# Half-row products on more array tiles, the gate in the sigmoid, five tiles ahead and turns at a bank

## The chip, the cores and the metric

One core of a Trainium2 chip runs the whole program. The metric is the time of one execution on the device, in microseconds (us). TensorE (PE) multiplies matrices, VectorE (DVE), ScalarE (ACT) and GpSimd (POOL) work element by element, and SyncE (SP) issues the transfers. Matrices stand in SBUF; products land in eight banks of PSUM, of 128 partitions by 512 numbers each.

## The reference

Two layers work on 512 tokens of 1024 numbers. Each has a mixer and a feed-forward, with norms, and with shifts, scales and gates that come from a condition vector. Layer 0's mixer is a sparse attention (an index product picks 128 keys per token); layer 1's is a state-space model. Cut to what matters here:

```python
x = x + g_m * mixer(h)                       # h = rms_norm(x) * (1 + scale) + shift
x = x + g_f * conv_ffn(h)

# mixer of layer 1: 64 groups of 16 channels, 64 complex states each, scanned along the tokens
bu = einsum('blgc,gpc->blgp', u, bb)
_, _, x_re, x_im = lax.associative_scan(...)
y = einsum(x_re, c_re) - einsum(x_im, c_im) + d_skip * u
g = gelu(y)
ga, gb = split(g @ w_glu)
out = ga * sigmoid(gb)

def conv_ffn(h):
    up = conv_along_tokens(h @ w_up, width=3) + conv_b     # 1024 -> 2 x 2816
    val, gate = split(up)
    return (silu(gate) * val) @ w_down
```

## The kernel before, in words

**Products.** The large products are made in three passes over operands that are split in a high and a low part (`mm3`: high x high, high x low, low x high); a row `acc<-wh,H` or `up<-H,wh` is of the first two, `wl` of the third. Small products are plain 32-bit ones; each of those matrix instructions leaves two records in the trace, so 16 matmuls are "x32" there.

**Order.** `Sched` (L172) writes the static order of every engine when the program is built. Tasks are generators that yield operations, spawned with a priority; `took` (L97) gives an operation's cost, `when` (L220) the time from which its operands are there in the scheduler's own model, from what `done` (L239) has noted of each region of a tile, and `run` (L322) picks, engine by engine, the operation that can start first, by priority. `Alt` names the same operation on two engines, and the scheduler takes the one where it ends sooner. Where the model sees PE idle for more than 1.6 us, `warm` (L751) puts in dummy products of the identity, tile `warm` in the trace. Nearly all instructions have the line of the scheduler's issue, L310, so they are told apart by tile names; `warm` has L759.

**Stages.** Attention: index product, selection, key and query products, 32 units (`unit`, L1062; tiles `S`, `s`, `pt`, `po`), output product. First feed-forward: `up` (L1202) makes one tile of 128 up-columns by 512 tokens in 24 matmuls; the first four tiles of a layer are taken together and in halves of 256 tokens, the first halves of all four before the second, since the norm's blocks of 128 tokens arrive one by one. Beside it run two side jobs of the SSM: `build_ops` (L1417) makes operators from the parameters, among them `kb`, a product of 64 rows by 32 columns per array tile, four tiles in one PSUM bank, with four copies `ks` on ACT.

**SSM.** `u_eight` gathers inputs (`pu`), `ssm_quarter` (L1740) makes for each of four quarters the inputs of the scan (`sre`), multiplies and scans them on DVE and POOL (`t`, `sre`) and leaves the states `X`. `ssm_out` (L1804) makes the outputs `py` of a quarter in two halves: a U part (8 matmuls) and an X part (16 matmuls on two array tiles of 64 x 64, one for each half of the rows); ACT takes gelu into `gy`, a gather `pg` turns it, and it becomes the operand H of the GLU. `load_states` (L1680) starts the loads for the quarters. `pre_ssm` (L1610), `scale_rows` (L1620) and `to_ssm` (L1636) bring the rows of a block through DRAM into the layout of the SSM.

**GLU.** Four products of 512 columns run in the order of `main` (L1873): gate half of the columns 0, value half 0, gate half 1, value half 1. `b_post` (L1850) takes the sigmoid of a gate block into `sg` on ACT. `a_post` (L1856) multiplies the value block by it on DVE, multiplies by the layer's gate vector on POOL, adds to x on DVE, and for the last columns starts the norm (`rs_v`, `rs_r`, `xn`) and the gathers `nt` of the second feed-forward's input H.

## Time and profile before

| | |
|---|---|
| median of 3 runs | 1280.53 us (1280.08 to 1280.97) |
| the profiled execution's own time | 1280.01 us |
| its span, first to last instruction | 1278.2 us |
| PE busy | 1252.0 us |
| DVE busy | 843.2 us |
| ACT busy | 520.6 us |
| POOL busy | 327.2 us |
| mean granted clock of PE | 0.995 |

The profile is one execution. A row of the timeline is a run of instructions of one kind on one engine: start, length, engine, line, operation, output<-input, shape, and how many records; in brackets how long the engine had been idle and what ended that. Ends of matmuls are modelled and overlap the next by a little, so the distance of two starts is the better measure. PE's granted clock is 1.00 at 2.4 GHz and 0.50 at 1.2 GHz.

### The profile page before, as it was taken

Reading aid. Unit: us, or ns where it says so; the run is one execution under the profiler, and the core shown is the slowest. Engines: PE = TensorE matmul, PEld = TensorE weight load, DVE = VectorE, ACT = ScalarE, POOL = GpSimd, SP = SyncE. Lnnn points to the kernel's source line nnn. Section 1 sums busy time; section 2 is a strip of 40 time slices with the busy share of each in tenths; the row PEclk is TensorE's granted clock in tenths of the full one; section 3 lists DMA queues with packets and bytes.
Section 4 is the critical chain, followed back from the end, with each engine's and each line's share of the span. In section 5 each row is a group of like instructions: output and inputs, shape, how many; then the busy total and the mean of one; then the engine's idle time right before and its main releaser. Section 6 shows DMA issues by size and latency. Waiting matters only on the chain. (4 is left out here: it accounts for less than half of the span.)

```text
span 1278.2 us, 19479 instructions
## 1 busy us (share of the span) xinstructions
PE 1252.0 (98%) x7264; PEld 989.7 (77%) x7264; DVE 843.2 (66%) x1602; ACT 520.6 (41%) x1121; POOL 327.2 (26%) x530
## 2 busy tenths in 40 slices
PE   7999999999999999999999999899999999999998
PEld 6766577666877678888888877788987888888886
DVE  6688697788677777768775378533686643666632
ACT  4345555556544334234443213423544432244420
POOL 0234446842144256343310304110200001000010
PEclk9999999999999999999999998999999999999999
DMA  9948521112386763444444669232443223322231
GB/s 375 365 162 316 179 85 64 53 34 67 118 304 242 245 237 113 143 176 144 153 126 177 158 197 372 91 104 77 165 137 138 97 91 124 114 77 77 81 99 48
DMA packets 76750, 195.68 MB, mean 153 GB/s; under 512 B 15204, under 2 KB 26084, under 8 KB 76656
## 3 DMA queue, kind: packets, MB, share of 16 engines
q1 hardware_dynamic: 73088, 191.52, 43.6%
q10 hardware_dynamic: 3568, 2.92, 0.8%
q8 instruction: 57, 0.93, 0.3%
q14 instruction: 37, 0.30, 0.1%
HBM read 172.10 MB, written 20.21 MB: 150 GB/s over the span
## 5 line engine op out<-in xcount | busy, mean ns | idle before, releaser
L310 PE MATMUL up<-H,wh 128*128 128x512 f32 (+1 forms) x1536 | 444.7, 374 | 0.0
L310 PEld LDWEIGHTS up<-H,wh 128*128 128x128 f32 x1536 | 277.7, 188 | 61.7 <-issue 12.1
L310 PE MATMUL up<-H,wl 128*128 128x512 f32 (+1 forms) x768 | 285.5, 372 | 0.0
L310 DVE TENSOR_TENSOR wl<-raw,wh 128x1024 fp32r<-128x1024 f32 (+1 forms) x192 | 234.2, 1227 | 65.5 <-ACT wh L310 59.4
L310 PE MATMUL acc<-wh,H 128*128 128x512 f32 (+3 forms) x752 | 241.1, 388 | 0.0
L310 ACT CAST wh<-raw 128x1024 fp32r<-128x1024 f32 (+1 forms) x192 | 192.7, 1015 | 109.9 <-DMA raw<-in_w_down_dram 45.8
L310 PE MATMUL acc<-wh,a 128*128 128x512 f32 x704 | 220.9, 392 | 0.0
L310 DVE SCALAR_TENSOR_TENSOR cv<-up,sm_b,cv 128x511 f32<-128x511 f32 (+1 forms) x176 | 131.6, 748 | 89.3 <-ACT cv L310 86.4
L310 PEld LDWEIGHTS acc<-wh,H 128*128 128x128 f32 x752 | 139.5, 189 | 44.2 <-issue 19.7
L310 PEld LDWEIGHTS up<-H,wl 128*128 128x128 f32 x768 | 144.6, 188 | 25.3
L310 PEld LDWEIGHTS acc<-wh,a 128*128 128x128 f32 x704 | 132.9, 189 | 27.8 <-issue 0.4
L310 ACT ACTIVATE cv<-up,sm_b 128x512 f32<-128x512 f32 x88 | 68.6, 780 | 197.5 <-PE up L310 180.0
L310 PE MATMUL acc<-wl,H 128*128 128x512 f32 (+3 forms) x376 | 141.7, 377 | 0.0
L310 POOL TENSOR_TENSOR x<-x,rt 128x512 f32<-128x512 f32 x20 | 31.5, 1578 | 415.7 <-DVE rt L310 407.6
L310 PE MATMUL acc<-wl,a 128*128 128x512 f32 x352 | 137.6, 391 | 0.0
L310 DVE TENSOR_TENSOR rt<-acc,gate 128x512 f32<-128x512 f32 x40 | 27.5, 689 | 101.0 <-PE acc L310 100.9
L310 PEld LDWEIGHTS acc<-wl,H 128*128 128x128 f32 x376 | 71.1, 189 | 10.2
L310 PEld LDWEIGHTS acc<-wl,a 128*128 128x128 f32 x352 | 66.4, 189 | 13.5
L310 POOL TENSOR_TENSOR rs_r<-rs_v,nhalf 128x1 f32<-128x1 f32 (+1 forms) x32 | 36.5, 1144 | 105.3 <-DVE rs_v L310 105.2
L310 ACT ACTIVATE cv<-cv 128x512 f32<-128x512 f32 x44 | 27.8, 632 | 68.5 <-DVE cv L310 68.5
L310 POOL TENSOR_TENSOR rm<-rm,rn 128x256 f32<-128x256 f32 (+3 forms) x46 | 37.2, 836 | 62.7 <-DVE rn L310 55.0
L310 PE MATMUL ada<-raw,cond_r 128*32 128x512 f32 (+1 forms) x544 | 49.2, 452 | 2.8 <-ACT xT L310 1.4
(268 smaller groups left out, 1512.9 us busy)
## 6 DMA issues: line engine op xcount, KB each, us to landing
raw<-in_ada_w_dram SPq DMA_DIRECT2D x96, 512.0 KB, 6.7
raw<-in_w_up_dram SPq DMA_DIRECT2D x88, 512.0 KB, 4.1
raw<-in_w_down_dram SPq DMA_DIRECT2D x40, 512.0 KB, 3.4
raw<-in_w_qkv_dram SPq DMA_DIRECT2D x24, 512.0 KB, 7.9
raw<-in_w_glu_dram SPq DMA_DIRECT2D x16, 512.0 KB, 9.6
k_d<-zq SPq DMA_DIRECT2D x8, 512.0 KB, 6.7
raw<-in_w_out_dram SPq DMA_DIRECT2D x8, 512.0 KB, 3.5
p_d<-p SPq DMA_DIRECT2D x16, 256.0 KB, 2.8
```

The source lines that it names most:

```text
L310: op.fn(*op.a, **op.k)
```

## The change

- **Costs of the scheduler.** A 32-bit product of 64 rows by at most 64 columns is priced at 0.55 of what it was. A PSUM bank that another engine reads counts as taken for readers of it until that read has ended (`when`, `done`, and `Res.get` with a fourth entry).
- **`kb`.** The 16 matmuls go to eight array tiles: two halves of the rows, each with a bank of its own, by four columns of 32. Eight copies of 32 x 128 follow instead of four of 32 x 256.
- **`py`.** Two banks instead of one, one for each half of the rows of the product; the outputs of neighbouring groups go to the two halves of the columns, so the X part has four 64 x 64 array tiles. Gelu comes in two instructions of 256 instead of one of 512. The rows of `w_glu` are laid out to match.
- **Gate.** The multiplication by the layer's gate vector moves from `a_post` to `b_post`, on POOL or DVE, onto the sigmoid.
- **Five tiles.** The first group of `up` has five tiles instead of four, in both layers.
- **Order of the SSM's start.** Sending the first half of a block's rows is a task of its own with a late priority, `scale_rows` of blocks 0 to 2 gets 2.5 instead of 0.8, and the states of quarters 0 and 1 are loaded under one rule.

```diff
@@ -108,6 +108,8 @@
             t = 0.013 + cols * 4.167e-4
         else:
             f = 1.0 if rhs.shape[0] > 64 and w > 64 else 0.285 if w <= 32 else 0.66
+            if rhs.shape[0] == 64 and w <= 64:
+                f *= 0.55
             if alone and f < 1:
                 f = 1.2
             t = max(0.056, f * cols * 4 * 4.167e-4 + 0.008)
@@ -222,8 +224,11 @@
         for aps, i in ((op.ins, 1), (op.outs, 2)):
             for ap in aps:
                 name, g = self.region(ap)
+
+                bank = ap.space == PSUM
                 for h, v in self.rec.get(name, {}).items():
-                    at = max(0.0 if op.e == v[2] == "PE" else v[0], v[1] if i == 2 else 0.0)
+                    at = max(0.0 if op.e == v[2] == "PE" else v[0],
+                             v[1] if i == 2 or bank and v[3] != op.e else 0.0)
                     if at > t and self.meet(g, h):
                         t = at
         return t
@@ -239,15 +244,15 @@
             name, g = self.region(ap)
-            v = self.rec.setdefault(name, {}).setdefault(g, [0.0, 0.0, ""])
-            v[1] = max(v[1], end)
+            v = self.rec.setdefault(name, {}).setdefault(g, [0.0, 0.0, "", ""])
+            v[1], v[3] = max(v[1], end), op.e
...
-            m[g] = [end, 0.0, op.e]
+            m[g] = [end, 0.0, op.e, ""]
@@ -1223,7 +1228,7 @@
         for half in range(2):
             i = 0
             while i < 2 * HT:
-                g = 4 if half == 0 and i == 0 else 1
+                g = 5 if half == 0 and i == 0 else 1
                 yield from up(2 * HT * half + i, g, 2 if g > 1 else 1)
                 i += g
                 flags.add(("up", layer, half))
@@ -1475,30 +1480,19 @@
                     tmp.put(Wt[h])
                     yield S.copy(p1[h].rearrange("p j i m -> p (j i m)"), pt)
                     sput(pt)
-                yield need(banks=1)
-                kb = sbank("kb")
-
-                ops = []
-                for ih in range(2):
-                    for i in range(2):
-                        for g2 in range(2):
-                            rows = slice(64 * g2, 64 * g2 + 64)
-                            for ip in range(2):
-                                ii = 2 * ih + ip
-                                jj = 4 * hq + ii
-                                qd = 64 * g2 + 32 * ip
-                                ops.append(PE.matmul(kb[qd:qd + 32, ih * P:(ih + 1) * P],
-                                                     bb[:, i].rearrange("p j c -> p (j c)")[rows, 16 * jj:16 * jj + 32],
-                                                     C[i][rows, ii, 0:8].rearrange("p k c -> p (k c)"),
-                                                     start=(i == 0), stop=(i == 1), tile_position=(64 * g2, qd)))
-                yield ops
+                yield need(banks=2)
+                kb = [sbank("kb") for _ in range(2)]
+
+                yield [PE.matmul(kb[g2][32 * ii:32 * ii + 32, :P],
+                                 bb[:, i].rearrange("p j c -> p (j c)")[64 * g2:64 * g2 + 64, 16 * (4 * hq + ii):16 * (4 * hq + ii) + 32],
+                                 C[i][64 * g2:64 * g2 + 64, ii, 0:8].rearrange("p k c -> p (k c)"),
+                                 start=(i == 0), stop=(i == 1), tile_position=(64 * g2, 32 * ii))
+                       for i in range(2) for ii in range(4) for g2 in range(2)]
                 jq = slice(4 * hq, 4 * hq + 4)
                 for g2 in range(2):
-                    for ip in range(2):
-                        qd = 64 * g2 + 32 * ip
-                        yield S.copy(ks[64 * g2:64 * g2 + 32, jq.start + ip:jq.stop:2],
-                                     kb[qd:qd + 32, :2 * P].rearrange("p (a b) -> p a b", a=2))
-                sput(kb)
+                    for ii in range(4):
+                        yield S.copy(ks[64 * g2:64 * g2 + 32, jq.start + ii], kb[g2][32 * ii:32 * ii + 32, :P])
+                sput(*kb)
                 spawn(store_ops(qt, jq, p1, C, ks, dB), 5.5)
 
     def ada1(*groups):
@@ -1613,6 +1607,9 @@
         yield need(tmps=1)
         xa = tmp.get("xa")
         yield Alt(*[E.tensor_mul(xa, x[:, b, :512], ROWS["a"][:, :512]) for E in (G, V)])
+        spawn(send_first(b, xa), 5.5)
+
+    def send_first(b, xa):
         yield DM(X8[0][16 * b:16 * b + 16], xa)
         tmp.put(xa)
         flags.add(("x0", b))
@@ -1640,7 +1637,7 @@
         r = yield from rstd_of(ss, 1, 1.0 / D, E0.pop(b))
-        spawn(scale_rows(b, r), 0.8)
+        spawn(scale_rows(b, r), 0.8 if b == NB - 1 else 2.5)
         yield V.scalar_tensor_tensor(xb, xb, r, ROWS["s"][:, 512:], op0=ALU.mult, op1=ALU.add)
@@ -1681,8 +1678,8 @@
             yield has(("built", q))
-            if q == 1:
-                yield lambda: WS.ns >= glu0 and len(U) and quad.free() >= 3
+            if q < 2:
+                yield lambda: WS.ns >= glu0 and len(U) >= 2 * q and quad.free() >= 3
@@ -1806,22 +1803,22 @@
         CA, Kt, own = OPS[q]
         for h in range(2):
             yield has(("x", q, h))
-            yield need(banks=1)
-            py = sbank("py")
+            yield need(banks=2)
+
+            py = [sbank("py") for _ in range(2)]
             js = range(4 * h, 4 * h + 4)
-            o = lambda j, g2: py[64 * g2:64 * g2 + 64, (j % 4) * P:(j % 4 + 1) * P]
-            ops = [PE.matmul(o(j, g2), U[q][:, 2 * j + g2], Kt[g2][:, j], start=(j == js[0]), stop=False,
-                             tile_position=(0, 64 * g2)) for j in js for g2 in range(2)]
-            for i in range(2):
-                for j in js:
-                    for g2 in range(2):
-                        r = slice(64 * g2, 64 * g2 + 64)
-                        ops.append(PE.matmul(o(j, g2), X[i][r, j], CA[i][r, j], start=False, stop=(i == 1 and j == js[-1]),
-                                             tile_position=(64 * g2, 64 * g2)))
-            yield ops
-            yield S.activation(gy[:, :, 4 * h:4 * h + 4].rearrange("p t j c -> p j t c"),
-                               py.rearrange("p (j t c) -> p j t c", j=4, t=8), AF.Gelu_apprx_tanh)
-            sput(py)
+            at = lambda j: 64 * (j % 2)
+            o = lambda j, g2: py[g2][at(j):at(j) + 64, j % 4 // 2 * P:(j % 4 // 2 + 1) * P]
+            yield [PE.matmul(o(j, g2), U[q][:, 2 * j + g2], Kt[g2][:, j], start=(j < js[2]), stop=False,
+                             tile_position=(0, at(j))) for g2 in range(2) for j in js]
+            r = [slice(64 * g2, 64 * g2 + 64) for g2 in range(2)]
+            yield [PE.matmul(o(j, g2), X[i][r[g2], j], CA[i][r[g2], j], start=False, stop=(i == 1 and j >= js[2]),
+                             tile_position=(64 * g2, at(j))) for i in range(2) for j in js for g2 in range(2)]
+            for g2 in range(2):
+                js_ = slice(4 * h + 2 * g2, 4 * h + 2 * g2 + 2)
+                yield S.activation(gy[:, :, js_].rearrange("p t j c -> p j t c"),
+                                   py[g2][:, :256].rearrange("p (j t c) -> p j t c", j=2, t=8), AF.Gelu_apprx_tanh)
+            sput(*py)
         flags.add(("y", q))
         quad.put(U[q])
         if own:
@@ -1847,19 +1844,24 @@
 
     sg = {}
 
-    def b_post(b, ps):
-        yield need(tmps=1)
-        sg[b] = tmp.get("sg")
-        yield S.activation(sg[b], ps, AF.Sigmoid)
-        bank.put(ps)
+    def b_post(ch):
+        def post(b, ps):
+            yield need(tmps=1)
+            s_ = tmp.get("sg")
+            yield S.activation(s_, ps, AF.Sigmoid)
+            bank.put(ps)
+
+            yield lambda: (1, 2) in gates
+            yield Alt(*[E.tensor_mul(s_, s_, gates[1, 2][:, ch * 512:(ch + 1) * 512]) for E in (G, V)])
+            sg[b] = s_
+        return post
 
     def a_post(ch, then):
         def post(b, ps):
-            yield lambda: b in sg and (1, 2) in gates
+            yield lambda: b in sg
             s_ = sg.pop(b)
             yield V.tensor_mul(s_, ps, s_)
             bank.put(ps)
-            yield G.tensor_mul(s_, s_, gates[1, 2][:, ch * 512:(ch + 1) * 512])
             xs = x[:, b, ch * 512:(ch + 1) * 512]
             yield V.tensor_add(xs, xs, s_)
             tmp.put(s_)
@@ -1973,12 +1975,12 @@
                     if k == KT - 1:
-                        spawn(b_post(b, acc[b]), 2)
+                        spawn(b_post(0)(b, acc[b]), 2)
...
         state["side_max"] = 3
         yield from gemm(KT, 512, gh[0], gh[1], a_post(0, None), tail=4)
-        yield from gemm(KT, 512, gh[0], gh[1], b_post, tail=4)
+        yield from gemm(KT, 512, gh[0], gh[1], b_post(1), tail=4)
         H1 = new_H()
@@ -2055,7 +2057,8 @@
-    wg = fp(f("ssm_w_glu")[0]).reshape(4, 8, 2, 16, 2, 2, 512).transpose(0, 2, 1, 3, 4, 5, 6).reshape(4, 2, 128, 2, 2, 512)
+    wg = fp(f("ssm_w_glu")[0]).reshape(4, 2, 2, 2, 2, 16, 2, 2, 512).transpose(0, 3, 1, 4, 2, 5, 6, 7, 8)
+    wg = wg.reshape(4, 2, 128, 2, 2, 512)
```

How the order moves, on PE, at three places. First the end of the SSM: the outputs `py` of quarter 2, the gathers `pg`, and the first GLU products `acc`. Before:

```order
L310 MATMUL pg<-sm_a,gy 128x128 x4
L310 MATMUL py<-XU,U 64x128 x8
L310 MATMUL py<-XU,X_8453 64x128 x8
L310 MATMUL py<-XU,X_8454 64x128 x8
L310 MATMUL ada<-raw,cond_r 32x512 x4
L310 MATMUL pg<-sm_a,gy 128x128 x4
L310 MATMUL acc<-wh,H 128x512
L310 MATMUL acc<-wl,H 128x512
L310 MATMUL acc<-wh,H 128x512 x2
L310 MATMUL acc<-wl,H 128x512
L310 MATMUL acc<-wh,H 128x512 x2
```

Now:

```order
L315 MATMUL py<-XU,U 64x128 x8
L315 MATMUL acc<-wh,H 128x512
L315 MATMUL acc<-wl,H 128x512
L315 MATMUL acc<-wh,H 128x512
L315 MATMUL py<-XU,X_8493 64x128 x8
L315 MATMUL py<-XU,X_8494 64x128 x8
L315 MATMUL pg<-sm_a,gy 128x128 x4
L315 MATMUL adat<-sm_a,rows 128x128 x4
L315 MATMUL acc<-wh,H 128x512
L315 MATMUL acc<-wl,H 128x512
L315 MATMUL acc<-wh,H 128x512
L315 MATMUL py<-XU,U 64x128 x8
```

GLU products, which stood behind both halves of quarter 2, now stand between its U and X parts. Up to the last `pg` of the stage there are 36 of them now and 30 before; behind that `pg` the change has a `warm` of 6.

Second, the passage from the GLU (`acc`) to the second feed-forward (`up`), with the gathers `nt` of the normed rows. Before:

```order
L310 MATMUL acc<-wh,H 128x512 x2
L310 MATMUL acc<-wl,H 128x512
L310 MATMUL acc<-wh,H 128x512
L310 MATMUL nt<-sm_a,xn 128x128 x4
L759 MATMUL warm<-sm_a 128x128 x17
L310 MATMUL up<-H,wh 128x256 x2
L310 MATMUL up<-H,wl 128x256
```

Now:

```order
L315 MATMUL acc<-wh,H 128x512
L315 MATMUL acc<-wl,H 128x512
L315 MATMUL acc<-wh,H 128x512 x2
L315 MATMUL acc<-wl,H 128x512
L315 MATMUL acc<-wh,H 128x512
L315 MATMUL nt<-sm_a,xn 128x128 x4
L315 MATMUL acc<-wh,H 128x512
L315 MATMUL acc<-wl,H 128x512
L315 MATMUL acc<-wh,H 128x512 x2
L315 MATMUL acc<-wl,H 128x512
L315 MATMUL acc<-wh,H 128x512
L315 MATMUL up<-H,wh 128x256 x2
```

Another gather stands in the row ahead of this piece. The last two gathers thus have six matmuls of the GLU behind each, where the last one had none, and no `warm` is left.

Third, the end of the attention's units: `S` are scores, `pt` transposes, `po` outputs, `acc<-wh,H` products of the input projection. Before:

```order
L310 MATMUL po<-pT,vt 64x128 x6
L310 MATMUL S<-kT,qT 128x512 x2
L759 MATMUL warm<-sm_a 128x128 x7
L310 MATMUL pt<-sm_a,s 128x128 x8
L310 MATMUL po<-pT,vt 64x128 x8
L310 MATMUL pt<-sm_a,s 128x128 x16
L310 MATMUL S<-kT,qT 128x512 x2
L310 MATMUL po<-pT,vt 64x128 x16
L310 MATMUL S<-kT,qT 128x128 x4
```

Now:

```order
L315 MATMUL acc<-wh,H 128x512
L315 MATMUL pt<-sm_a,s 128x128 x8
L315 MATMUL acc<-wh,H 128x512
L315 MATMUL acc<-wl,H 128x512
L315 MATMUL acc<-wh,H 128x512
L315 MATMUL po<-pT,vt 64x128 x8
L315 MATMUL pt<-sm_a,s 128x128 x8
L315 MATMUL acc<-wh,H 128x512
L315 MATMUL acc<-wl,H 128x512
L315 MATMUL acc<-wh,H 128x512
L315 MATMUL po<-pT,vt 64x128 x8
```

Products of the input projection reach down to here and stand between the transposes and the outputs. The `warm` of 7 is gone; one of 8 stands further up, within that projection.

## Rows read from the trace of the kernel before

**Rows 1.** Page, part 1: busy time, share of the span and instructions of each engine.
```profile
PE 1252.0 (98%) x7264; PEld 989.7 (77%) x7264; DVE 843.2 (66%) x1602; ACT 520.6 (41%) x1121; POOL 327.2 (26%) x530
```

**Rows 2.** Waits of PE over the span: us in total, times, longest.
```profile
PE pg L310 <- ACT gy L310: 3.6, 1, 3.6
...
PE po L310 <- DVE pT L310: 1.6, 5, 0.5
...
PE pt L310 <- DVE s L310: 1.4, 2, 0.9
```

**Rows 3.** Timeline, PE, three stretches: start, us, engine line op out<-in xcount [idle before].
```profile
250.52 1.83 PE L759 MATMUL warm<-sm_a 128*128 128x128 f32 x14
...
363.43 1.28 PE L759 MATMUL warm<-sm_a 128*128 128x128 f32 x10
...
906.35 3.96 PE L759 MATMUL warm<-sm_a 128*128 128x128 f32 x34
```

**Rows 4.** Windows: us, then PE, PEld, DVE, ACT, POOL busy (x), PEclk, DMA share, GB/s.
```profile
776.20:783.10 6.90, 6.90 (x62) 6.01 (x60) 5.00 (x8) 2.96 (x4) 1.42 (x4) 0.51 1.03 403
806.90:810.40 3.50, 2.96 (x9) 2.57 (x10) 3.41 (x5) 1.12 (x3) 2.80 (x2) 0.51 0.02 5
```

**Rows 5.** Timeline, PE, the SSM stage's end and the GLU's start.
```profile
780.50 3.17 PE L310 MATMUL py<-XU,X 64*64 64x128 f32 x32
...
807.44 1.12 PE L310 MATMUL pg<-sm_a,gy 128*128 128x128 f32 x4 [3.58 <-ACT gy L310]
...
825.76 0.40 PE L310 MATMUL acc<-wl,H 128*128 128x512 f32 x1
```

**Rows 6.** Timeline, PE, one `kb` group in the first feed-forward.
```profile
387.72 1.08 PE L310 MATMUL kb<-C,bb 64*32 64x128 f32 x32
388.72 0.73 PE L310 MATMUL up<-H,wh 128*128 128x512 f32 x2
```

**Rows 7.** Windows, of the first feed-forward and of the SSM stage.
```profile
380.00:440.00 60.00, 60.00 (x351) 42.10 (x350) 44.56 (x89) 24.52 (x37) 23.96 (x58) 1.00 0.73 240
785.50:800.00 14.50, 14.43 (x242) 11.68 (x238) 13.87 (x20) 5.36 (x9) 6.30 (x5) 1.00 1.03 402
```

**Rows 8.** Groups of instructions that read tile `kb`, on ACT: ns min/median/max, first and last start.
```profile
L310 ACT COPY ks<-kb x32: 344/364/367, 390.5 to 659.4; 32x256 f32<-32x256 f32 x32
```

**Rows 9.** Timeline, PE, `py` of quarter 3, first half.
```profile
813.23 1.09 PE L310 MATMUL py<-XU,U 128*64 128x128 f32 x16
814.26 1.96 PE L310 MATMUL py<-XU,X 64*64 64x128 f32 x32
816.15 0.66 PE L310 MATMUL adat<-sm_a,rows 128*128 128x128 f32 x4
```

**Rows 10.** Timeline, DVE, the SSM stage.
```profile
785.62 1.29 DVE L310 TENSOR_TENSOR t<-sre,T 128x512 f32<-128x512 f32 x2 [2.08 <-PE sre L310]
```

**Rows 11.** Timeline, POOL, X of quarter 3.
```profile
808.89 2.21 POOL L310 TENSOR_TENSOR X<-t,t 128x504 f32<-128x504 f32 x1 [0.63 <-DVE t L310]
```

**Rows 12.** Chain that ended last: start, us, engine tile line xcount.
```profile
895.80 0.44 PE nt L310 x4
...
963.28 70.95 PE up L310 x312
```

**Rows 13.** Timeline, POOL, then DVE, end of the GLU.
```profile
894.56 1.73 POOL L310 TENSOR_TENSOR sg<-sg,gate 128x512 f32<-128x512 f32 x1 [1.78 <-DVE sg L310]
...
896.32 0.69 DVE L310 TENSOR_TENSOR x<-x,sg 128x512 f32<-128x512 f32 x1 [1.18 <-POOL sg L310]
...
898.34 0.69 DVE L310 TENSOR_TENSOR H<-ht,H 128x512 fp32r<-128x512 f32 x1
```

**Rows 14.** Timeline, PE, the first `up` of layer 1.
```profile
910.07 0.48 PE L310 MATMUL up<-H,wh 128*128 128x256 f32 x2
...
910.50 0.40 PE L310 MATMUL up<-H,wh 128*128 128x256 f32 x2
...
910.86 0.40 PE L310 MATMUL up<-H,wh 128*128 128x256 f32 x2
```

More of the change, by code (lines that the diff above doesn't have):

```diff
@@ L391, in get @@
         ap = self.pool.tile(shape or [P, self.cols], dtype, tag=self.tag, bufs=self.n, name=name)
-        self.s.rec[ap.tensor.name] = {(0, P, 0, 1 << 40, ()): [at, 0.0, ""]}
+        self.s.rec[ap.tensor.name] = {(0, P, 0, 1 << 40, ()): [at, 0.0, "", ""]}
         return ap
```

## The prediction

> **What bounds the kernel now.** I read the page first: TensorE (PE) is busy 98% of the span and the other engines 66% or less [rows 1]. So two things can make the kernel shorter: PE executing its matmuls in less time, and PE no longer standing still. The table of waits says how little of the second is left by name: the longest after the start is 3.6 us before a gather `pg`, and the two entries of the attention's units come to 1.6 and 1.4 us over all 32 of them [rows 2]. But "busy" hides two more kinds of waste, so I read the timeline and the windows next. Padding: the scheduler puts `warm` matmuls where it foresees idleness; three of their rows, at 250, 363 and 906 us, come into the sum [rows 3]. Half clock: two stretches of the SSM stage have a granted clock of 0.51, which is the 1.2 GHz level [rows 4]; in the second, PE had just stood 3.58 us in front of `pg` [rows 5]. The durations below are taken from rows at the full 2.4 GHz where nothing else is said.
>
> The profiled execution took 1280.01 us, its span is 1278.2 and the median of the runs is 1280.53, so sums made against 1280.0 hold for the median within half a microsecond. Under 0.2% (2.6 us) a measurement of this kernel can't tell a difference from none.
>
> **Part 1, `kb` on eight array tiles.** Eight groups of 32 records run between products of the feed-forward. One starts at 387.72, and the next row starts 1.00 us later [rows 6]. Today four tiles work at a time: 8 steps of 125 ns. If eight tiles run together at that pace there are 4 steps, 0.5 us, and PE is the bound there, its windows full (60.00 of 60 us) [rows 7]. Taken: 0.45 us each, **-3.6** in all; bounds 0 (no more overlap) and -4.0. The four more copies per group go to ACT, 24.52 of 60 us busy there [rows 7], and are costed at nothing; without that cover a group's copies would be four more of the 0.36 us that one takes now [rows 8], at most 8 x 4 x 0.36 = 11.5 us, but only if PE had no `up` to go on with.
> The same row gives a second reading. 32 records in 1.00 us is 31 ns a record, and no group of the trace shows less. The Trainium skill, *TensorE: Matmul & The Clock Gate*, section "Wait — 56ns, not 53.3ns?", says that matmuls never start closer than about 25 ns apart, however small they are; no run here has shown that floor yet. By it (an estimate from that page) `kb` would end at 0.8 us and the term would be -1.6; it is a rival below.
>
> **Part 2, the end of the SSM and the GLU's start.** The X part of a half takes 1.89 us from 814.26 to 816.15 with two tiles at work, 59 ns a record [rows 9]. On four quadrants it is 32 records at `kb`'s four-tile pace of 31 ns [rows 6]: 1.0 us, 0.9 saved in each of eight halves. Only where PE is the limit does it count. In quarter 0 it does: `sre` of quarter 2 waits behind that product, and DVE waits 2.08 us for `sre` at 785.62 [rows 10]; from there it is 13.87 of 14.50 us busy up to 800 [rows 7], and what it does is the chain to quarter 3's X. The X of this half, at 780.50, ran at half clock and took 3.17 us [rows 4, 5], so 0.9 to 2.0 is gained, within the 2.08 that DVE has idle. X of quarter 3 is ready at 811.10 now (808.89 + 2.21, on POOL) [rows 11]; I take 809.5 to 811.1 for the change, middle 810.3.
> From there I count progress. Before, 30 GLU matmuls stand ahead of the stage's last `pg`, and the 36th is the row at 825.76, done by 826.0 [rows 5]. After, the order has all 36 ahead of that `pg`, 24 of them between quarter 2's products, where PE now stands for 3.58 us. What is left behind quarter 3's X: two X parts of 1.0, one U part (813.23 to 814.26 now, 1.0) [rows 9], twelve GLU matmuls at the 0.227 of a 512-column product [rows 12] (2.7), two `pg` of four records and 6 `warm` of two, 20 records at the 0.11 of `warm` (2.2): 7.9 us. The 36th is then done at 818.2: **-7.8**. The padding is part of it, and so is the half clock of rows 4, which the filled hole should prevent. Bounds: if DVE and POOL are the limit and a last gather waits for gelu as now, some 3 to 5 us of that comes back: -3; with X at 808.5, -10.
> `load_states` and the priorities only set the order of this stage. The 13 `warm` in place of 20 ahead of the first `sre` stand in a hole that a norm's chain sets: nothing.
>
> **Part 3, the gate in the sigmoid.** At the end of the GLU POOL multiplies a block by the gate in 1.73 us, and the sum on DVE waits for it until 896.32 [rows 13]. The first `up` starts at 910.07 [rows 14], behind the `warm` that starts at 906.35 [rows 3], 3.7 us (34 records, 0.11 each). The order of the change has no `warm` there: two gathers `nt` stand among the last GLU matmuls, then `up`. PE's work up to there is the same, so `up` can start at 906.35, **-3.7**. It needs the first half of block 1's H then, and the second after the first four steps of a tile (12 matmuls at 0.12: 1.4 us, 907.8). The last `nt` now comes 6 matmuls earlier, ends near 905.0, and from the end of the `nt` of 895.80 [rows 12] to the end of its H at 899.03 [rows 13] it is 2.8 us: 907.8. Just in time; if it is not, at most 1.4 comes back, so the bounds are -2.3 and -4. The multiply itself is hidden: it is done once the sigmoid is there, many microseconds ahead of the product that needs it, on POOL and DVE.
>
> **Part 4, five tiles ahead, twice.** The fifth tile's 24 matmuls of 512 become 48 of 256. Three halves take 0.36 us (910.50 to 910.86) [rows 14], so 0.12 each; a full one takes 70.95 / 312 = 0.227 [rows 12]. 24 x (0.24 - 0.227) = 0.3, in two layers **+0.6**. For that PE has 2.9 us more to do ahead of the second half of the columns: in layer 0 the 1.28 us of `warm` at 363.43 [rows 3] go, **-1.3**, bounds -1.3 and +1 (H late, a bare wait in its place); in layer 1 it is cover for part 3.
>
> **Part 5, turns at a bank.** The rule costs no instruction; it changes the order of the attention. Its `warm` of 1.83 us at 250.52 goes [rows 3], and 8 new ones (16 records x 0.11) come in the input projection: 0. The waits in the attention's units add to 3.0 us [rows 2]; I take half as gone, **-1.5**, bounds -3 and +5 (0.15 us more in each of 32 units). PE changes ten times more between the two kinds of product and back. A change costs little: `up` behind `kb` takes 0.57 us for two at 388.72 [rows 6] where 0.45 is the rule, so 0.1 a pair, **+1.0**.
>
> **Sum**: -3.6 - 7.8 - 3.7 + 0.6 - 1.3 - 1.5 + 1.0 = -16.3. I give 0.8 back for what the exact fits of parts 2 and 3 can miss: -15.5, **1264.5 us**.
>
> **The rivals.**
> A, *an issue floor*: small matmuls start no closer than some interval, whatever tiles they use. For it: no row shows less than 31 ns. Against: none of them had eight tiles to use. `kb` goes to 0.8 us, -1.6 in place of -3.6, X (31 ns) hardly changes: 1266.5. The skill's page has this rule. Chance 0.14.
> B, *tiles of one row half don't run together*: neither `kb` nor X changes its pace. For it: X is at 59 ns with two tiles, and nothing in the trace shows four 64x64 tiles. Against: `kb`'s four tiles stand at 31 ns. It costs 3.6 of part 1 and 1.8 (quarter 3) plus about 1 (quarter 0) of part 2: 1271. Chance 0.10.
> C, *the SSM stage is DVE's and POOL's*: the wait moves from `pg` to X of quarter 3 or the gather behind it, and the clock falls again. For it: DVE's 13.87 of 14.50 us [rows 7], POOL's 2.21 us for one X [rows 11]. Against: just before, DVE waits 2.08 us for PE [rows 10]. Part 2 gives 1.5 instead of 7.8: 1270.8. Chance 0.18.
> D, *slower*: the new order of the attention opens waits. The scheduler now believes in turns that the chip may not have, and puts a unit's products behind each other. Each unit would wait more than 15.5 / 32 = 0.48 us longer, at which point all gain is gone; at 0.6 it is +19: 1283.7. Against: all waits there are 3.0 us now, 0.1 a unit [rows 2], so they would have to grow sixfold. Chance 0.07.
> E, *nothing*: the tiles wait for each other as before and every hole moves on to the next engine, with the span half a microsecond shorter: 1279.5. For it: DVE's load. Against: the `warm` rows of 906 and 363 are bare PE time that the order no longer has. Chance 0.03.
>
> **How the numbers follow.** The forecast has 0.48. Faster by over 0.2% are it, A, B and C: 0.90, less 0.01 for ends of C: 0.89. E and the edges of C and D make the same: 0.05; slower: 0.06. The range: the low end takes the good bounds of parts 2 and 5 (2.2 and 1.5), `kb`'s 0.4 and some 3 us for attention and joins that fit better than I counted: 1257. The upper end takes in A, B and C with two to three more us: 1274. D and E are left out, with some 0.1 of tails.
>
> **What would show it.** `kb` rows: 0.5 us to the next row (A: 0.8, B: 1.0). X rows of `py`: 1.0 us for 32 records (B: 1.9). No 3.58 us in front of a `pg` and no clock of 0.51 around 808; the 36th GLU matmul 7.8 us nearer to the end of the first feed-forward than now (C: a wait of 3 us or more, before X or `pg`). No `warm` and no wait over 0.5 us between the last GLU matmul and `up`; none at the first feed-forward's join. The sum of PE's waits in 100 to 260 us under 5 us (D: over 15). The prediction is wrong if the attention's span up to 265 us grows by more than 5 us, or if the SSM stage from the end of the first feed-forward to the GLU's 36th matmul shrinks by less than 3.

## The result, and the profile after

The changed kernel takes 1267.42 us (median of 4 runs, 1265.99 to 1271.37), the kernel before 1280.75 (median of 4): a ratio of 0.9892, with a 95% interval of 0.9871 to 0.9912. That is 13 us faster; the time is 2.9 us above the 1264.5 that was forecast, and inside the range. The profiled execution took 1268.01 us, 12.0 less than the profiled one before, and it is those 12.0 that the stages below divide.

Two of the first lines of the changed kernel's page (compare [rows 1]):

```profile
span 1266.2 us, 19526 instructions
...
PE 1239.3 (98%) x7268; PEld 975.8 (77%) x7268; DVE 838.0 (66%) x1584; ACT 531.3 (42%) x1166; POOL 323.5 (26%) x545
```

PE is as full as before, with 12.7 us less to do. Where they went is read from the start of the same product in both profiles:

| from | to | before | after | difference | forecast |
|---|---|---|---|---|---|
| start | first `up` | 348.26 | 351.90 | **+3.6** | -1.5, and a part of the +1.0 for switches |
| first `up` | last product of the first feed-forward | 406.23 | 401.70 | -4.5 | -3.6 - 1.3 + 0.3 |
| there | 100th GLU product | 85.38 | 77.68 | -7.7 | -7.8 |
| there | first `up` of layer 1 | 70.20 | 67.00 | -3.2 | -3.7 |
| there | last product | 363.13 | 362.94 | -0.2 | +0.3 |

The products that bound the stages, on PE, before and then after (the first `up` of layer 1 before is in [rows 14], the one after stands further down):

```profile
348.26 0.40 PE L310 MATMUL up<-H,wh 128*128 128x256 f32 x2
...
754.49 0.40 PE L310 MATMUL acc<-wh,a 128*128 128x512 f32 x1
...
839.87 0.39 PE L310 MATMUL acc<-wh,H 128*128 128x512 f32 x1
...
1273.20 0.39 PE L310 MATMUL acc<-wh,a 128*128 128x512 f32 x1
...
351.90 0.40 PE L315 MATMUL up<-H,wh 128*128 128x256 f32 x2
...
753.60 0.39 PE L315 MATMUL acc<-wh,a 128*128 128x512 f32 x1
...
831.28 0.39 PE L315 MATMUL acc<-wh,H 128*128 128x512 f32 x1
...
1261.22 0.39 PE L315 MATMUL acc<-wh,a 128*128 128x512 f32 x1
```

Four stages came as forecast within half a microsecond; the first moved the other way. Here are the lines that show it. Waits of PE over the span (compare [rows 2]: `pg` had 3.6, `pt` 1.4):

```profile
PE pt L315 <- DVE s L315: 4.2, 2, 3.0
PE pu L315 <- DVE t L315: 3.5, 2, 3.1
...
PE pg L315 <- ACT gy L315: 1.4, 2, 1.1
```

The 3.6 us ahead of `pg` have shrunk, as expected, and a wait of 3.0 us in the attention is the new longest one. The timeline of PE there, and of DVE:

```profile
262.44 0.71 PE L315 MATMUL S<-kT,qT 64*128 64x128 f32 x8
266.11 2.22 PE L315 MATMUL pt<-sm_a,s 128*128 128x128 f32 x10 [2.96 <-DVE s L315]
...
262.86 1.22 DVE L315 TENSOR_TENSOR wl<-raw,wh 128x1024 fp32r<-128x1024 f32 x1
...
265.47 0.88 DVE L315 TENSOR_SCALAR s<-s,rsm 128x512 f32<-128x512 f32 x2
```

PE waits for the scaled scores `s`, which DVE makes at 265.47; a split of weights (`wl`) and four masks of the next units stand ahead of them on DVE. Windows of the changed kernel, behind that wait, in the SSM stage, and where the clock fell in [rows 4] at 806.90:

```profile
266.40:269.80 3.40, 3.40 (x23) 2.90 (x22) 1.96 (x6) 0.43 (x2) 1.19 (x2) 0.50 0.01 2
775.00:781.80 6.80, 6.80 (x80) 6.02 (x81) 3.68 (x6) 3.94 (x7) 0.82 (x3) 0.50 1.04 404
803.00:808.00 5.00, 4.12 (x33) 3.27 (x33) 5.00 (x9) 3.69 (x7) 3.19 (x2) 1.00 0.14 52
```

The half clock at 776 is still there, the one around 808 is gone, and one stands in the attention. The prediction counted two stretches of half clock before; there is a third, of 3.4 us, in the first feed-forward near 738, in both kernels. The rest of the profile answers to the forecast's steps. `kb` (compare [rows 6]), the SSM's end (compare [rows 5, 9]) and the passage to the second feed-forward (compare [rows 3, 14]), on PE:

```profile
394.64 0.67 PE L315 MATMUL kb<-C,bb 64*32 64x128 f32 x32
395.24 0.73 PE L315 MATMUL up<-H,wh 128*128 128x512 f32 x2
...
808.17 1.10 PE L315 MATMUL py<-XU,X 64*64 64x128 f32 x32
809.21 1.09 PE L315 MATMUL py<-XU,U 128*64 128x128 f32 x16
...
814.83 0.39 PE L315 MATMUL acc<-wh,H 128*128 128x512 f32 x1
815.06 0.60 PE L315 MATMUL pg<-sm_a,gy 128*128 128x128 f32 x4
815.50 1.50 PE L764 MATMUL warm<-sm_a 128*128 128x128 f32 x12
816.76 0.48 PE L315 MATMUL acc<-wh,H 128*128 128x512 f32 x1
...
898.05 0.40 PE L315 MATMUL acc<-wh,H 128*128 128x512 f32 x1
898.28 0.40 PE L315 MATMUL up<-H,wh 128*128 128x256 f32 x2
```

`kb` takes 0.60 us for 32 records, X 1.04. The 36th GLU product, at 814.83, is followed by a gather and the padding, and `up` begins 0.23 us after the last GLU product.

### The profile page after: what moved, and what is told of

The parts are those of the page before. It is cut to its first block, busy times and chain, and to the rows that moved or that the text cites. A ratio compares the mean times of both kernels' runs of the same rounds, so it can differ in the third digit from the quotient of the medians.

```text
span 1266.2 us, 19526 instructions
## 1 busy us (share of the span) xinstructions
PE 1239.3 (98%) x7268; PEld 975.8 (77%) x7268; DVE 838.0 (66%) x1584; ACT 531.3 (42%) x1166; POOL 323.5 (26%) x545
## 5 line engine op out<-in xcount | busy, mean ns | idle before, releaser
L315 PEld LDWEIGHTS up<-H,wh 128*128 128x128 f32 x1568 | 281.7, 189 | 61.4 <-issue 10.4
L315 PE MATMUL acc<-wh,H 128*128 128x512 f32 (+3 forms) x752 | 244.2, 389 | 0.0
L315 PEld LDWEIGHTS up<-H,wl 128*128 128x128 f32 x784 | 147.7, 188 | 24.6
L315 PEld LDWEIGHTS acc<-wh,a 128*128 128x128 f32 x704 | 132.9, 189 | 27.8 <-issue 0.2
L315 ACT ACTIVATE cv<-cv 128x512 f32<-128x512 f32 x44 | 27.8, 632 | 68.9 <-DVE cv L315 68.9
L315 POOL TENSOR_TENSOR rm<-rm,rn 128x256 f32<-128x256 f32 (+3 forms) x46 | 33.9, 763 | 59.0 <-DVE rn L315 57.9
```

Source lines behind the costliest of these rows:

```text
L315: op.fn(*op.a, **op.k)
```

## The experiments

Each run is compared by the stages of the table, each from one profile. Two profiles of the changed kernel agree within a tenth from the first index product on; what moves a stage without any edit is above all the clock. Up to the first index product PE has the same instructions in all 14 profiles, and that took 61.2 to 62.3 us in those with full clock near 20 us and 62.9 to 65.1 in those with 3.4 to 6.8 us of half clock there. In the first feed-forward 11 of the 14 profiles, those of before and after among them, have half clock near 738 (between 732 and 750), in all but one 3.4 us of it; its second product with `w_down` then took 65.3 to 66.8 us, and 64.0 to 64.1 in the three without (`no_turn`, `four`, `old_py`). The medians carry this too. Ratios are to the kernel before on the same chip.

**The rule of turns, taken out altogether** (`no_turn`).

```diff
-                             v[1] if i == 2 or bank and v[3] != op.e else 0.0)
+                             v[1] if i == 2 else 0.0)
```

> The changed kernel without the rule of turns at a bank (the scheduler's readiness no longer looks at the last reader of a bank; all else as changed). Theory 1, the rule's new order costs time in the attention: the first `up` comes at about 348.3 us as in the kernel before, not at 351.9, there is no wait of 2.96 us before `pt` near 266 and no half clock there, and the time is about 1264.4 us (1268.0 less 3.6). Rival, the rule pays over the whole program: the attention gets shorter but waits for gelu or copies come back in the SSM stage and the GLU, and the time is 1268 us or more.

Measured: 1269.62 us, ratio 0.9904 (0.9884 to 0.9924). From the first index product to the first `up` it took 288.6 us (changed kernel 290.7, before 287.1), with a half clock at 266.3 all the same. And the SSM stage took 81.3 us in place of 77.7. (The first feed-forward was 1.5 us shorter; this profile has no half clock near 738.) Two lines of PE's waits that the changed kernel doesn't have, both in the SSM stage, and a window there:

```profile
PE py L315 <- POOL X L315: 1.8, 1, 1.8
PE acc L315 <- ACT H L315: 1.4, 1, 1.4
...
809.10:812.40 3.30, 3.30 (x22) 2.35 (x19) 0.99 (x3) 0.66 (x2) 0.00 (x0) 0.50 0.45 154
```

The expected clock in the attention was wrong, and the rival was right in this: the rule costs in the attention and pays 3.6 us in the SSM stage, where the order that it makes is what keeps PE from standing for X and H.

**The rule from the first feed-forward on** (`late_turn`).

```diff
+LATE = 360.0
...
-                bank = ap.space == PSUM
+                bank = ap.space == PSUM and self.free["PE"] > LATE
```

> The changed kernel with the rule of turns at a bank in force only after 360 us of the scheduler's own clock, so for the feed-forwards, the SSM and the GLU but not for the attention. Theory 1: first `up` at about 348.3 us and about 1264.4 us in all; against the run without the rule at all the difference is what the rule gives in the SSM stage and the GLU (0 to 2 us). Rival: what the attention wins is lost again at the first feed-forward's start, where the halves of the norm then arrive late: the end of the first feed-forward stays at 753.6 us and the time at 1268.

Measured: 1266.79 us, 0.9881 (0.9860 to 0.9902). The attention's order is that of the kernel before, and so is all of it but the clock: 288.7 us, with 0.50 from 267.6 to 270.9. The SSM stage takes 77.68 us, the changed kernel's value to the hundredth. So 2.0 us are what the order costs there (290.7 against 288.7, both with a half clock). Against `no_turn` the rule gives 3.6 us in the SSM stage, more than the 0 to 2 of theory 1. The median is not clearly apart from the changed kernel's. The window:

```profile
267.60:270.90 3.30, 3.28 (x20) 2.62 (x22) 1.81 (x10) 0.86 (x3) 3.05 (x18) 0.50 0.10 16
```

**The kernel before and the changed one, profiled again** (no edit).

> The kernel before, profiled once more, to compare stages on the same chip. If the half clock that the changed kernel shows at 266 to 270 us comes from its own longer wait there, this profile has none between 250 and 290 us and takes 287.1 us from the first index product to the first `up`, as the first profile of it did. If the half clock there comes and goes by itself, it may show here too, and the stage then takes about 1.7 us more.

> The changed kernel once more, on the same chip as the one with the dummy matmuls in the attention, so that the two can be set against each other. If the rule of turns costs 2 us of waits there and brings the half clock with it each time, this profile again shows a wait of 2.9 us near 266, a clock of 0.51 behind it, and 290.7 us from the first index product to the first `up`.

Measured: before 287.2 us, full clock in 250 to 290, time 1281.34; changed 290.7 us, half clock from 269.3, with this wait, time 1270.61, 0.9906 (0.9890 to 0.9923):

```profile
269.33 2.37 PE L315 MATMUL pt<-sm_a,s 128*128 128x128 f32 x10 [2.96 <-DVE s L315]
```

In all eight profiles that have the changed kernel's attention the clock fell there; with the old order it fell in two of five (the two runs above), and then cost 1.6 us (288.7 and 288.6 against 287.1). So of the 3.6 us 2.0 are waits and 1.6 are clock; the order of before runs the same risk, and the new one met it each time.

**Dummy matmuls ahead of the attention's waits** (`att_warm`), on `late_turn`.

```diff
+    LEAD = {("pt", 25): 2, ("po", 13): 1, ("pt", 31): 4, ("po", 16): 2}
...
+            for _ in range(LEAD.get((kind, count[kind]), 0)):
+                nc.tensor.matmul(tile_[:, :P], ident, ident, start=True, stop=True)
```

`LEAD` says how many products of the identity go ahead of the n-th group of that name.

> The kernel with the rule of turns in force from the feed-forward on (late_turn), and nine dummy matmuls (2.0 us of PE at full clock) directly ahead of the four transposes and outputs near 255 and 265 us for which PE stands 0.45, 0.35, 0.95 and 0.48 us. Nothing else is moved. Theory 1, the clock falls there because PE stands so often: no clock of 0.51 between 250 and 290 us, 287.1 us from the first index product to the first `up`, and a time 1 to 2 us under the changed kernel's on this chip. Rival, the dummies keep no clock up or push back what stands behind them: 288.6 us or more.

Measured: 1263.40 us, 0.9858 (0.9838 to 0.9878). The stage takes 287.1 us; windows and timeline of PE there:

```profile
250.00:290.00 40.00, 39.33 (x296) 27.36 (x292) 32.73 (x120) 21.64 (x70) 19.47 (x79) 1.00 0.09 29
...
261.58 1.16 PE L1079 MATMUL pt<-sm_a 128*128 128x128 f32 x8
262.58 0.32 PE L1080 MATMUL pt<-sm_a,s 128*128 128x128 f32 x1
```

Its interval ends at 0.9878, and the changed kernel's on the same chip begins at 0.9890. Of the 7.3 us between the two profiled executions the attention's stage explains 3.6 (287.1 against 290.7). Another 3.0 lie ahead of the first index product, where the instructions are the same; the changed kernel's profile had the half clock there and this one had not, so that part is no gain of the dummies. That the dummies hold the clock up is likely but not shown: without them the same order had a full clock in three of five profiles.

**`kb` as before** (`old_kb`): one bank, four tiles, four copies.

```diff
-                yield need(banks=2)
-                kb = [sbank("kb") for _ in range(2)]
+                yield need(banks=1)
+                kb = sbank("kb")
...
+                                                     start=(i == 0), stop=(i == 1), tile_position=(64 * g2, qd)))
```

> The changed kernel with `kb` as before: four tiles, one bank, four copies. Theory 1, `kb` is PE time with nothing beside it: a group takes 1.0 us instead of 0.6, the first feed-forward ends 3.3 us later (8 x 0.41) and the time is about 1271.3 us. Rival: the end of the first feed-forward is set by side jobs on DVE and ACT, so that the time stays at 1268 us.

Measured: 1275.88 us, 0.9950 (0.9932 to 0.9969). The first feed-forward takes 5.5 us longer (407.2 against 401.7). A group takes 1.00 us again, which for eight makes 3.3. A wait of 1.55 that the forecast didn't have, as the scheduler set one `kb` ahead of its operand, makes that group 1.95 us longer still; 0.2 stay unexplained. (Another 3.9 us of this profile lie ahead of the first index product, with half clock there.) The first group, and the one that waits:

```profile
399.08 1.08 PE L315 MATMUL kb<-C,bb 64*32 64x128 f32 x32
400.08 0.73 PE L315 MATMUL up<-H,wh 128*128 128x512 f32 x2
...
641.96 0.63 PE L315 MATMUL kb<-C,bb 64*32 64x128 f32 x14 [1.55 <-DVE C L315]
```

So `kb`'s own price is 3.3 us, and most of the rest is the order that came out.

**`kb` in pairs** (`kb_pairs`).

```diff
-                       for i in range(2) for ii in range(4) for g2 in range(2)]
+                       for ih in range(2) for i in range(2) for ii in (2 * ih, 2 * ih + 1) for g2 in range(2)]
```

> The changed kernel, `kb` in the same two banks with the same eight copies, but the matmuls in the order of pairs: four array tiles take their two products each, then the other four. Theory 1, the pace comes from the number of tiles at work: a group takes 1.0 us as before the change, 8 steps of 125 ns. Rival, the pace comes from the second bank, or from the rate at which matmuls start: 0.6 us as in the changed kernel.

Measured: one run, 1270.0 us. The first `kb`:

```profile
395.18 0.69 PE L315 MATMUL kb<-C,bb 64*32 64x128 f32 x32
395.81 0.72 PE L315 MATMUL up<-H,wh 128*128 128x512 f32 x2
```

0.63 us, not 1.0: the forecast of theory 1 was wrong. The single records say why the run was no test of it: four start within 20 ns, the next four begin 54 ns after the first, and then each four starts anew every 109 to 134 ns. So it seems that the second four tiles didn't wait for the first to do their second product, and that all eight worked; the trace does not name the tile of a record, so this is read from the distances. Whether the second bank is needed for that pace wasn't separated: eight tiles in one bank would put both row halves on the same partitions.

**The two-tile `ssm_out`** (`old_py`: `ssm_out` and the rows of `w_glu` as before), and the same without the five `warm` that the scheduler then put between `pu` and `py` (`old_py_bare`).

```diff
-            py = [sbank("py") for _ in range(2)]
+            py = sbank("py")
...
-            if e == "PE" and self.warm and at - self.free[e] > 1.6:
+            if e == "PE" and self.warm and at - self.free[e] > 1.6 and not 745 < at < 765:
```

> The changed kernel with `ssm_out` as before: two array tiles for the X part, one bank, gelu in one instruction of 512 (and the rows of the GLU's weights laid out for that). Theory 1, PE's time for X counts where quarter 3 and quarter 0 stand on the path: X takes 1.9 us for 32 records again, and from the last product of the first feed-forward to the 100th of the GLU it takes 80 to 81 us (77.7 in the changed kernel, 85.4 before); the time is 2.5 to 3.5 us above the changed kernel's. Rival, the stage is bound by DVE and POOL and the order alone brought the gain: the stage stays within 0.5 us of 77.7.

> The kernel with the two-tile `ssm_out` once more, less the 5 dummy matmuls that the scheduler had put between `pu` and `py` of quarter 0. The stage from the first feed-forward's last product to the 100th of the GLU took 82.8 us with them against 77.7 in the changed kernel. Theory 1, the dummies (2.4 us at half clock) stood on the path by themselves and X's pace is worth 2 to 3 us: the stage takes 80 to 81 us. Rival, X's pace is worth all of it: still 82.3 to 82.8 us, with PE waiting or at half clock instead of the dummies.

Measured: 1275.45 us, 0.9945 (0.9927 to 0.9964), SSM stage 82.8; bare 1275.46, 0.9944 (0.9929 to 0.9959), SSM stage 81.5. Two lines of PE in the bare one, at half clock:

```profile
782.64 3.05 PE L315 MATMUL py<-XU,X 64*64 64x128 f32 x32
785.61 2.09 PE L315 MATMUL sre<-U,p 128*64 128x64 f32 x64
```

So the four-tile form (tiles, two banks and two gelu instructions together) is worth 3.8 us of the stage (81.5 against 77.7), more than the 2 to 3 of theory 1 and less than the rival's 4.6 to 5.1, and the padding 1.3. The two medians are alike all the same. In the profiles, the padded kernel lost 3.1 us in the attention, with 10.3 us of half clock in place of 3.4, and won 3.4 us ahead of the first index product and 1.8 in the first feed-forward, where the bare one had half clock and it had none.

**The gate back in the chain** (`old_gate`: `b_post` and `a_post` as before).

```diff
-            yield Alt(*[E.tensor_mul(s_, s_, gates[1, 2][:, ch * 512:(ch + 1) * 512]) for E in (G, V)])
...
+            yield G.tensor_mul(s_, s_, gates[1, 2][:, ch * 512:(ch + 1) * 512])
```

> The changed kernel with the multiplication by the gate vector back in the chain behind the value product (POOL only). Theory 1: 17 `warm` stand again ahead of the second layer's `up`, the last GLU product to the first `up` takes 4.4 us instead of 0.2, two gathers of 0.44 us no longer stand among the products, and the time is about 1271.3 us. Rival, five tiles of cover are enough by themselves: 1268 us with no wait at the join.

Measured: 1273.96 us, 0.9935 (0.9918 to 0.9952). The padding is back, and 70.2 us lie between the 100th GLU product and `up`, the value of before; five tiles alone don't cover it:

```profile
901.12 3.96 PE L764 MATMUL warm<-sm_a 128*128 128x128 f32 x34
904.84 0.48 PE L315 MATMUL up<-H,wh 128*128 128x256 f32 x2
```

**Four tiles in the first group** (`four`).

```diff
-                g = 5 if half == 0 and i == 0 else 1
+                g = 4 if half == 0 and i == 0 else 1
```

> The changed kernel with four tiles in the first group of `up`. Theory 1, the fifth tile is cover at the first feed-forward's start alone: 5 `warm` (1.1 us) come back there, 0.3 us of split matmuls go in each layer, and with the gate out of the chain the second layer needs no more cover: the time is within 1 us of the changed kernel's. Rival, four tiles end before the last block's H in the second layer: a wait of 2 us or more there, and 2 to 3 us above the changed kernel's.

Measured: 1271.26 us, 0.9917 (0.9895 to 0.9939). In the second layer nothing waits for more than 0.2 us and the feed-forward takes 0.1 us more, not less. In the first the 10 records of `warm` come back, and the first half of `up` takes 150.4 us in place of 147.5, of which 0.9 is a wait of `ada` for a transfer at 453.6, a product that the fifth tile does not feed. The whole first feed-forward takes 403.0 us, 2.4 to 2.7 more than the other two profiles without half clock near 738 (400.6 and 400.2); less the 0.9 that leaves 1.5 to 1.9 for the fifth tile. The interval overlaps the changed kernel's, so the stage alone speaks.

**Dummy matmuls ahead of `pu`** (`pu_warm`), on `late_turn`, placed directly ahead of the first transpose of the second `pu`.

```diff
+                for _ in range(12):
+                    nc.tensor.matmul(pu[:, :P], ident, ident, start=True, stop=True)
```

> The kernel with the rule of turns in force from the feed-forward on (late_turn), and 12 dummy matmuls on PE directly ahead of the second `pu`, where PE stands for 2.8 us and then runs at half clock for 6.8 us. Nothing else is moved. Theory 1, the half clock follows the standing and PE's work there is on the path: no clock of 0.51 between 774 and 784 us, and the stage up to the 100th GLU product takes 75 to 76 us instead of 77.7. Rival, DVE's and POOL's chain sets the stage: the clock stays full but the stage still takes 77.2 to 77.7 us and PE waits longer ahead of `pg`.

Measured: 1265.61 us, 0.9868 (0.9847 to 0.9889). Half of the half clock went (what is left is from 775.6 to 779.0), and PE's standing shrank to 0.72 us:

```profile
768.31 2.94 PE L1732 MATMUL pu<-sm_a 128*128 128x128 f32 x24
771.97 0.32 PE L1733 MATMUL pu<-sm_a,XU 64*128 64x64 f32 x1 [0.72 <-DMA XU<-xb]
```

The stage still took 78.0 us, 0.3 more than in `late_turn`. But the run doesn't price the half clock. Counted from the last product of the first feed-forward, the transposes began 0.8 us later than in `late_turn`, behind the transfer named in the row above; the half clock that was left lay on the U and X products of quarter 0; and `sre` of quarter 2 began at 28.3 us and not at 27.8. So PE came no earlier, and theory 1 was not put to the test. What speaks for the rival is the changed kernel's own trace. DVE, which before waited 2.08 us for that `sre` [rows 10], now takes it without a wait, stands once for 0.35 us for an H, and from 785 to 812 never for more than 0.11:

```profile
783.91 0.68 DVE L315 TENSOR_TENSOR t<-sre,T 128x512 f32<-128x512 f32 x1
784.93 0.63 DVE L315 TENSOR_TENSOR H<-pg,H 128x256 fp32r<-128x256 f32 x1 [0.35 <-ACT H L315]
```

In `att_warm`, `old_gate` and `kb_pairs`, which don't have this wait, the stage takes 77.2 to 77.4 us. So with DVE's order as it is, up to half a microsecond is what a faster PE could give there, which is an estimate from these profiles. The median is lower than that of `late_turn`, but in the profiles that is the attention, which kept the full clock (287.1 us), and 2.1 us ahead of the first index product, so it is no proof for the dummies.

## Why the prediction was right, and where it was off

*Part 1, -3.6.* Right: 0.60 us in place of 1.00, 8 x 0.41 = -3.3; the run with the old `kb` gives as much back. Rival A falls: 32 records in 0.60 us are 18.7 ns each, and records start 7 ns apart within a bunch. The trace of before had this already: in its `kb` four records start at 0, 7, 13 and 20 ns, and the next four from 133 on. The 31 ns of the prediction is the mean over a group, so "no row shows less" was no evidence for a floor. By the Trainium skill's 25 ns (*TensorE: Matmul & The Clock Gate*, "Wait — 56ns, not 53.3ns?") the group would have ended at 0.8 us, an estimate; the measurement decides against it here. Rival B falls with X at 1.04 us for 32 records on four quadrants.

*Part 2, -7.8.* Right in size, -7.7, but in part because errors cancelled. The sum took the row at 825.76 for the 36th GLU product; counted in the trace it is the 38th, and the 36th was done at 825.5, 0.5 us earlier. Counted from the end of the first feed-forward, X of quarter 3 started on PE 1.2 us ahead of the 810.3 assumed. From that start to the 37th GLU product it took 8.6 us and not 7.9. Together that is -7.9 up to the 37th product, of which 0.2 went again up to the 100th.

The two causes named are there: X's pace, within the four-tile form that the bare run prices at 3.8 us, and GLU products in the hole ahead of `pg`, with no half clock around 808. But one thing speaks against the part's first place for it, quarter 0: in the bare run, with two tiles, POOL had X of quarter 3 ready 54.4 us behind the end of the first feed-forward, with four 54.7, before 56.6. The 3.8 us arose behind that X, where PE in the bare run stands nowhere for over 0.1 us. And the part credited the filled hole to the order as such. The run without the rule shows that it is the rule of turns that makes this order: without it 3.6 of the 7.7 are gone again. Part 5 therefore priced the rule in the wrong place. No run took out both the rule and the four-tile form, so whether their 3.6 and 3.8 add up is open; and none put back the order of the SSM's start or the new price of a 64-row product, so what these do is not separated. Rival C had this much of the truth that after the change DVE no longer waits for PE there.

*Part 3, -3.7.* Right: -3.2 from the 100th GLU product to `up`, given back whole by `old_gate`. The missing 0.5 is a gather: five `nt` now stand ahead of `up`, four did before, 0.44 us that moved from behind it, which is also why the second feed-forward shows -0.2 and not +0.3.

*Part 4, -0.7.* Right within some tenths: of the -4.5 of the first feed-forward 3.3 are `kb`, and the other 1.2 stand against -1.3 + 0.3. `four` gives the fifth tile 1.5 to 1.9 there, so the agreement is no finer than that. In layer 1 the part took the tile as cover for part 3; `four` shows that with the gate out of the chain no cover is needed.

*Part 5, -1.5 + 1.0.* Wrong, and the step is "I take half as gone": the waits of the attention's units were to shrink, and one of 2.96 us came, with a half clock behind it: +3.6 us for the stage, inside the bounds of -3 and +5. The mechanism is that of rival D, at one place in place of 32: the new order put work of DVE ahead of what PE needed. 2.0 of the 3.6 are the order's; the 1.6 of the clock came with it in every profile, but fell in two of five with the old order too. The +1.0 for switches between products was not measured by itself. Those 3.6 us, against a forecast of -0.5 for the two terms, are nearly the whole of the gap between -16.3 and -12.0.

## What to carry to other kernels

A rule in a scheduler is a change of every stage: price it stage by stage, and try it in one stage and not in the other, as here it took 2.0 us in one, 3.6 with the clock that fell behind the wait, and gave 3.6 in another. Padding is worth removing where PE is the path: between the GLU and `up` 3.7 us of it were 3.2 us of time there and 0.4 behind it. Where another engine is without a pause, ask how long that engine waits for PE: in the SSM stage it was 0.35 us. And compare two profiles only after you have set their stretches of half clock side by side; here these alone moved a stage by up to 4 us. Small products spread over more array tiles gain nearly in proportion to the tiles at work, as long as other products of PE stand ready behind them.

## What the runs showed of the hardware

A step of a 64-row product with 128 columns took PE about 109 ns at full clock, with two, four or eight tiles at work, and about 213 at half clock (X of quarter 0). A record then costs 59 (X before), 32 (X after) and 18.7 ns (`kb` after). A tile that is still busy did not hold back records for other tiles behind it, as far as the starts tell (`kb` in pairs). The same instructions of PE in the same order had a granted clock of 1.00 in one profile and 0.50 for 3.4 us in another, at a place where PE stands four times for 0.35 to 0.95 us within 12 us (`late_turn`). And the clock also fell where PE did not stand: near 738 in the changed kernel, behind 3.8 us of 64x64 transposes `pu`, with no idle time of PE on record in the feed-forward up to there:

```profile
732.91 3.77 PE L315 MATMUL pu<-sm_a,XU 64*128 64x64 f32 x32
...
737.50:740.90 3.40, 3.40 (x10) 2.63 (x9) 2.37 (x5) 0.72 (x2) 0.55 (x1) 0.51 0.64 238
```
